# The sums of w_ada moved from GpSimd and ScalarE to VectorE in a two-layer diffusion backbone

## The chip, the cores and the metric

The kernel runs on one core of a Trainium2 chip. The metric is the device time of one execution in microseconds (us); the median of three runs before the change is 1243.5 us (1242.24 to 1245.1). TensorE (PE) does the matrix products, VectorE (DVE), ScalarE (ACT) and GpSimd (POOL) the element work, and SyncE (SP) issues most DMA transfers. Each engine takes its instructions from its own queue, in order.

## The reference

Two layers run over 512 latent tokens of width 1024. Layer 0 mixes tokens by attention and a Fourier transform, layer 1 by a conformer convolution module; each layer ends with a gated feed-forward part of width 2816 with a short convolution. Before each part the tokens are normalised, scaled and shifted, and behind it they are gated. The six vectors of each layer that scale, shift and gate come from one conditioning vector:

```
def ada_params(cond, w_ada_i, b_ada_i):
    m = jax.nn.silu(cond) @ w_ada_i + b_ada_i
    ...
    return jnp.split(m, 6, axis=-1)
...
        x_lat = x_lat + g1 * o_lat
        h = modulate(rmsnorm(x_lat, g_ffn[i]), sh2, sc2)
        x_lat = x_lat + g2 * conv_ffn(h, w_up[i], w_fdw[i], b_fdw[i], w_down[i])
```

`silu(cond) @ w_ada` is a product of one row with a 1024 x 6144 matrix for each layer. The kernel reads w_ada from HBM in tiles of 128 x 1024: a tile holds 128 output columns, one for each partition, and along its free dimension all 1024 inputs. Multiplied by silu(cond), which stands in every partition (tile `scb`), and summed along the free dimension, one tile gives 128 values of one vector; eight tiles give a vector.

## The kernel before, in words

**Weights.** All other weights come as 174 chunks of 128 x 1024 (`Stream`). The DMA of a chunk goes to one of two stage tiles `st`; ScalarE rounds it to its high part `whi` (L195), and VectorE takes the low part `wlo = st - whi` (L196). Five chunks are held at a time, so chunk n+5 is made when TensorE is done with chunk n. A product takes three matmuls (`mm3`, L223 to L225): high by high, high by low, low by high. A chunk is 24 matmuls of 512 columns. The text calls chunks by their number in this stream, which is also the number in the names `whi33`, `wlo33`.

**The feed-forward part of layer 0, ffn(0).** Chunks 18 to 21 are its first block. Then come, for each i, two "up" chunks (22 and 23, 24 and 25, 26 and 27, 29 and 30, ...), whose results TensorE puts into PSUM banks `B`, of which there are four in rotation. Every second i has a "down" chunk between (28, 33, 38, ...), whose results gather in the wide tiles `D`. When an up chunk is done, `conv` runs on its bank: one pass on ScalarE (L923) and two on VectorE (L924, L925); the second VectorE pass frees the bank for the up chunk four banks later. `glu` multiplies the two halves (L933), and a down chunk needs the result g split into a high part (ScalarE, L290) and a low part (VectorE, L291). Behind chunk 32 the gate takes two banks of the rotation, so that chunk 34 gets the bank of chunk 31 and chunk 35 that of chunk 32.

**The sums.** `ada_sum` loads a tile of w_ada into `sa` (three buffers, SyncE queue), GpSimd multiplies it by `scb` in place (L384), and ScalarE sums each half along the row (L387, two instructions, each followed by a read of its accumulator). At the end VectorE adds the pairs and the bias (L390, L391). 40 tiles run in ffn(0), 8 in the conformer part, 8 in ffn(1), always as fillers beside the products. A gate is wanted in every row: `in_every_row` spreads a vector by 8 small matmuls on TensorE (L369), four into each of two banks, and ScalarE copies each bank out (L370).

**The conformer part.** Up chunks 84 to 99 are followed by a convolution by transforms; among it two tiles `bp` of a bias are loaded into the same two stage tiles `st` as the weights, multiplied on GpSimd by the gate, and added to x by eight GpSimd instructions (L1143), after which the stage tiles are free again.

**What sets the order.** The program is written in loops with fillers, but the framework's scheduler puts the instructions of each engine into a fixed order when the program is built. So the order of a queue is settled before the run, and an instruction that is not ready holds all behind it.

## Time and profile before

| | before |
|---|---|
| median of the runs | 1243.5 us |
| profiled execution | 1242.08 us, span 1240.3 us |
| TensorE busy | 1172.2 us (95%) |
| VectorE busy | 764.1 us (62%) |
| ScalarE busy | 588.1 us (47%) |
| GpSimd busy | 260.3 us (21%), of it 153.9 us on the 56 multiplications L384 |

The profile gives each engine's instructions with start and duration, what an engine waited for, and the granted clock of TensorE as a share of full speed (PEclk). Busy shares are averages; the stretches that matter here are 300 to 450 us (ffn(0) with 40 sums), 690 to 765 us (conformer with 8) and 895 to 930 us (ffn(1) with 8).

### The profile page before, as it was taken

The page shows a single profiled execution, that of the slowest core. Times are in us where ns is not written, and L with a number is a line of the kernel's source. Part 1 is how long each engine was busy: PE and PEld are TensorE (multiplying, and loading weights), DVE is VectorE, ACT ScalarE, POOL GpSimd, SP SyncE. Part 2 cuts the span into 40 slices and gives each one's busy share as a digit, 9 for nine tenths or more (in the row PEclk, how much of TensorE's full clock was granted, in tenths as well). Part 3 has the DMA queues.
Part 4 walks back from the last instruction along what each step waited for, and adds up shares of the span by engine and source line. Part 5 has one row for each costly group of instructions (what it writes and reads, how often), then busy time and mean ns, then how long its engine had stood idle before and what let it go on. Part 6 is the DMA issues. An engine that isn't in the chain of part 4 may idle for free.

```text
span 1240.3 us, 15425 instructions
## 1 busy us (share of the span) xinstructions
PE 1172.2 (95%) x5813; PEld 962.7 (78%) x5813; DVE 764.1 (62%) x1092; ACT 588.1 (47%) x1021; POOL 260.3 (21%) x164
## 2 busy tenths in 40 slices
PE   4899899999996999999999999979999999999998
PEld 1686477769885888888888877868988888888886
DVE  3458599346987667554646675664686545555563
ACT  4454587325766664334444543342574433433441
POOL 2025255001677830000001650000250000000000
PEclk8999999999998999999999998989999999999999
DMA  9534600222666653222234443101264232232230
GB/s 361 219 135 160 204 1 1 99 105 86 244 224 238 228 206 133 100 89 101 86 102 154 156 139 105 55 17 51 86 207 132 85 103 88 99 102 92 95 119 34
DMA packets 43834, 156.43 MB, mean 126 GB/s; under 512 B 5008, under 2 KB 5520, under 8 KB 43504
## 3 DMA queue, kind: packets, MB, share of 16 engines
q1 hardware_dynamic: 42192, 149.51, 34.9%
q0 software_dynamic: 1120, 5.54, 1.3%
q8 instruction: 46, 0.75, 0.2%
q10 hardware_dynamic: 448, 0.39, 0.1%
q14 instruction: 28, 0.23, 0.1%
HBM read 153.33 MB, written 2.10 MB: 125 GB/s over the span
## 4 chain that ended last, share of the span: by engine, by line
PE 73%; DVE 10%; DMA 7%; ACT 4%; issue 3%; POOL 2%; SPq 0%; POOLq 0%; ACTq 0%; DVEq 0%
PE B L223 17%; PE B L224 16%; PE B L225 16%; PE D L223 6%; PE D L224 6%; PE D L225 6%; DVE wlo L196 3%; DMA sa<-in_wada_dram 3%; DMA st<-in_wall_dram 2%; POOL sa L384 2%; PE B L829 2%; PE B L338 1%; DMA wn<-in_wnat_dram 1%; DVE tiny L809 1%; ACT P L812 1%
## 5 line engine op out<-in xcount | busy, mean ns | idle before, releaser
L196 DVE TENSOR_TENSOR wlo<-st,whi 128x1024 fp32r<-128x1024 f32 x174 | 239.2, 1378 | 245.0 <-ACT whi L195 242.0
L223 PE MATMUL B<-h,whi 128*128 128x512 f32 (+1 forms) x880 | 313.8, 370 | 10.9 <-DVE tmp L925 8.8
L224 PE MATMUL B<-h,whi 128*128 128x512 f32 (+1 forms) x880 | 321.8, 369 | 0.0
L225 PE MATMUL B<-h,wlo 128*128 128x512 f32 (+1 forms) x880 | 320.3, 368 | 0.0
L195 ACT CAST whi<-st 128x1024 fp32r<-128x1024 f32 x174 | 182.1, 1049 | 177.2 <-PE B L224 101.7
L223 PEld LDWEIGHTS B<-h,whi 128*128 128x128 f32 x880 | 162.3, 190 | 39.2 <-issue 9.4
L224 PEld LDWEIGHTS B<-h,whi 128*128 128x128 f32 x880 | 167.2, 190 | 26.8
L225 PEld LDWEIGHTS B<-h,wlo 128*128 128x128 f32 x880 | 166.8, 190 | 27.1
L384 POOL TENSOR_TENSOR sa<-sa,scb 128x1024 f32<-128x1024 f32 x56 | 153.9, 2767 | 79.1 <-DMA sa<-in_wada_dram 39.1
L290 ACT CAST g<-g 128x512 fp32r<-128x512 f32 x88 | 54.6, 621 | 153.6 <-DVE g L933 74.4
L287 POOL TENSOR_TENSOR tiny<-tiny,mhalf 128x1 f32<-128x1 f32 (+3 forms) x26 | 21.2, 816 | 462.4 <-DVE tiny L286 461.2
L291 DVE TENSOR_TENSOR g<-g,g 128x512 fp32r<-128x512 f32 x88 | 69.9, 795 | 71.4 <-ACT g L290 71.4
L387 ACT ACTIVATE sa<-sa 128x512 f32<-128x512 f32 x112 | 69.5, 624 | 30.3 <-POOL sa L384 30.1
L224 PE MATMUL D<-wlo,g 128*128 128x512 f32 x176 | 68.5, 389 | 0.0
L225 PE MATMUL D<-whi,g 128*128 128x512 f32 x176 | 68.5, 389 | 0.0
L223 PE MATMUL D<-whi,g 128*128 128x512 f32 x176 | 68.5, 389 | 0.0
L223 PE MATMUL B<-whi,g 128*128 128x512 f32 x176 | 68.5, 389 | 0.0
L224 PE MATMUL B<-wlo,g 128*128 128x512 f32 x176 | 68.5, 389 | 0.0
L225 PE MATMUL B<-whi,g 128*128 128x512 f32 x176 | 67.8, 389 | 0.0
L924 DVE SCALAR_TENSOR_TENSOR tmp<-B,vecs,tmp 128x511 f32<-128x511 f32 x84 | 62.1, 743 | 5.3 <-ACT tmp L923 5.3
L931 ACT ACTIVATE tmp<-tmp 128x512 f32<-128x512 f32 x44 | 27.8, 631 | 77.9 <-DVE tmp L925 77.1
L923 ACT ACTIVATE tmp<-B,vecs 128x512 f32<-128x512 f32 x84 | 64.4, 771 | 0.0
(239 smaller groups left out, 1919.5 us busy)
## 6 DMA issues: line engine op xcount, KB each, us to landing
st<-in_wall_dram SPq DMA_DIRECT2D x174, 512.0 KB, 3.5
sa<-in_wada_dram SPq DMA_DIRECT2D x56, 512.0 KB, 4.4
wn<-in_wnat_dram SPq DMA_DIRECT2D x24, 512.0 KB, 9.3
sa<-in_wnat_dram SPq DMA_DIRECT2D x16, 512.0 KB, 4.8
x<-in_x_dram SPq DMA_DIRECT2D x4, 512.0 KB, 5.2
dft<-in_dft_dram POOLq DMA_DIRECT2D x2, 1024.0 KB, 6.9
out_dram<-x SPq DMA_DIRECT2D x8, 256.0 KB, 2.0
scb<-in_cond_dram SPq DMA_DIRECT2D x3, 512.0 KB, 5.7
```

The costliest lines, as they stand in the source:

```text
L195: nc.scalar.copy(hi, st)
L196: nc.vector.tensor_tensor(out=lo, in0=st, in1=hi, op=ALU.subtract)
L223: nc.tensor.matmul(out, lhsT=lh, rhs=rh, start=start, stop=False)
L224: nc.tensor.matmul(out, lhsT=lh, rhs=rl, start=False, stop=False)
L225: nc.tensor.matmul(out, lhsT=ll, rhs=rh, start=False, stop=stop)
L290: nc.scalar.copy(hi, src)
L291: nc.vector.tensor_tensor(out=lo, in0=src, in1=hi, op=ALU.subtract)
L384: nc.gpsimd.tensor_tensor(out=st, in0=st, in1=cur["c"], op=ALU.mult)
L387: nc.scalar.activation(out=u, in_=u, func=AF.Identity, accum_out=acc[:, 2 * kt + i : 2 * kt + i + 1])
L923: nc.scalar.activation(out=y, in_=b, func=AF.Identity, scale=w[:, 1:2], bias=vec(f"bfdw{l}", i))
L924: nc.vector.scalar_tensor_tensor(out=y[:, 1:SEQ], in0=b[:, 0 : SEQ - 1], scalar=w[:, 0:1], in1=y[:, 1:SEQ], op0=ALU.mult, op1=ALU.add)
L931: nc.scalar.activation(out=sa, in_=ya, func=AF.Silu)
```

## The change

GpSimd no longer takes part. For each tile of w_ada one VectorE instruction multiplies it by `scb` and sums along the row (`scalar_tensor_tensor` with `accum_out`, L384 after). ScalarE's two sums per tile go, and so does the pairwise addition L390. `acc` has 8 columns and six buffers. A gate is spread in two steps of the filler, one bank each.

```
-    def in_every_row(col, dst):
-        for half in range(2):
+    def in_every_row(col, dst, halves=(0, 1)):
+        for half in halves:
...
-        acc = tp.tile([P, KT * 2], F32, tag="asum", name=nm("asum"), bufs=3)
+        acc = tp.tile([P, KT], F32, tag="asum", name=nm("asum"), bufs=6)
         for kt in range(KT):
             st = chunk_tile()
             nc.sync.dma_start(st, wada[(6 * l + j) * KT + kt])
-            nc.gpsimd.tensor_tensor(out=st, in0=st, in1=cur["c"], op=ALU.mult)
-            for i in range(2):
-                u = st[:, i * 512 : i * 512 + 512]
-                nc.scalar.activation(out=u, in_=u, func=AF.Identity, accum_out=acc[:, 2 * kt + i : 2 * kt + i + 1])
+            nc.vector.scalar_tensor_tensor(out=st, in0=st, scalar=1.0, in1=cur["c"], op0=ALU.mult, op1=ALU.mult, accum_out=acc[:, kt : kt + 1])
             yield
         col = tiny(8)
-        nc.vector.tensor_reduce(out=col, in_=acc.rearrange("p (k s) -> p k s", s=2), op=ALU.add, axis=AX.X)
-        nc.vector.tensor_tensor(out=col, in0=col, in1=vec("ba", (6 * l + j) * KT, KT), op=ALU.add)
+        nc.vector.tensor_tensor(out=col, in0=acc, in1=vec("ba", (6 * l + j) * KT, KT), op=ALU.add)
         yield col
...
-                in_every_row(col, dst)
+                in_every_row(col, dst, (0,))
+                yield
+                in_every_row(col, dst, (1,))
```

The scheduler's order changes with it. After the change every line from L396 on has a number lower by two (L924, L925, L933 and L1143 before are L922, L923, L931 and L1141 after).

VectorE at the start of the sums in ffn(0), before: low parts of chunks 23 to 26 and the conv passes of the first block (banks B_624 to B_626).

```order
L196 TENSOR_TENSOR wlo23_2996<-st23_2997,whi23_2995 128x1024
L924 SCALAR_TENSOR_TENSOR tmp_628_3019<-B_624_2799,vecs_70,tmp_628_3019 128x511
L196 TENSOR_TENSOR wlo24_3002<-st24_3003,whi24_3001 128x1024
L925 SCALAR_TENSOR_TENSOR tmp_628_3019<-B_624_2799,vecs_70,tmp_628_3019 128x511
L924 SCALAR_TENSOR_TENSOR tmp_630_3025<-B_625_2800,vecs_70,tmp_630_3025 128x511
L924 SCALAR_TENSOR_TENSOR tmp_631_3030<-B_626_2801,vecs_70,tmp_631_3030 128x511
L925 SCALAR_TENSOR_TENSOR tmp_630_3025<-B_625_2800,vecs_70,tmp_630_3025 128x511
```

The same place after, with the sums (sa, asum) among them:

```order
L384 SCALAR_TENSOR_TENSOR sa_639_3114,asum_638_3113<-sa_639_3114,scb_621_2794 128x1024
L384 SCALAR_TENSOR_TENSOR sa_640_3117,asum_638_3113<-sa_640_3117,scb_621_2794 128x1024
L384 SCALAR_TENSOR_TENSOR sa_646_3193,asum_638_3113<-sa_646_3193,scb_621_2794 128x1024
L196 TENSOR_TENSOR wlo23_2996<-st23_2997,whi23_2995 128x1024
L922 SCALAR_TENSOR_TENSOR tmp_628_3019<-B_624_2799,vecs_70,tmp_628_3019 128x511
L196 TENSOR_TENSOR wlo24_3002<-st24_3003,whi24_3001 128x1024
L384 SCALAR_TENSOR_TENSOR sa_647_3196,asum_638_3113<-sa_647_3196,scb_621_2794 128x1024
L384 SCALAR_TENSOR_TENSOR sa_659_3312,asum_638_3113<-sa_659_3312,scb_621_2794 128x1024
L923 SCALAR_TENSOR_TENSOR tmp_628_3019<-B_624_2799,vecs_70,tmp_628_3019 128x511
L384 SCALAR_TENSOR_TENSOR sa_660_3315,asum_638_3113<-sa_660_3315,scb_621_2794 128x1024
```

Three sums now stand ahead of chunk 23's low part, and further ones between each pair of the old instructions.

VectorE further on in ffn(0), after: the second conv pass on bank B_668 (chunk 31) and what stands between it and that on B_669 (chunk 32), which comes twelve rows later. These are the banks that chunks 34 and 35 take over.

```order
L923 SCALAR_TENSOR_TENSOR tmp_674_3497<-B_668_3397,vecs_70,tmp_674_3497 128x511
L384 SCALAR_TENSOR_TENSOR sa_797_4777,asum_770_4498<-sa_797_4777,scb_621_2794 128x1024
L931 TENSOR_TENSOR g32_622_2797<-tmp_664_3384,tmp_665_3386 128x512
L196 TENSOR_TENSOR wlo38_3492<-st38_3493,whi38_3491 128x1024
L384 SCALAR_TENSOR_TENSOR sa_840_5147,asum_839_5146<-sa_840_5147,scb_621_2794 128x1024
L387 TENSOR_TENSOR tiny_807_4891<-asum_770_4498,vecs_70 128x8
L922 SCALAR_TENSOR_TENSOR tmp_676_3503<-B_669_3398,vecs_70,tmp_676_3503 128x511
L291 TENSOR_TENSOR g_693_3669<-g32_622_2797,g_692_3668 128x512
L384 SCALAR_TENSOR_TENSOR sa_845_5188,asum_839_5146<-sa_845_5188,scb_621_2794 128x1024
L196 TENSOR_TENSOR wlo39_3549<-st39_3550,whi39_3548 128x1024
L384 SCALAR_TENSOR_TENSOR sa_850_5229,asum_839_5146<-sa_850_5229,scb_621_2794 128x1024
```

The next two rows are the first conv pass of chunk 34 and then the second of chunk 32, the 35th sum being the last one ahead of them. In the order of before no sum stands on this engine.

TensorE in ffn(0), after: the end of chunk 29, then part of down chunk 33, then chunk 30. Before, chunk 30 follows chunk 29 at once, and all of chunk 33 stands behind chunk 32.

```order
L223 MATMUL B_661_3318<-h_5_86,whi29_3146 128x512
L224 MATMUL B_661_3318<-h_6_87,whi29_3146 128x512
L225 MATMUL B_661_3318<-h_5_86,wlo29_3147 128x512
L223 MATMUL D_654_3269<-whi33_3295,g_670_3459 128x512
L223 MATMUL D_655_3270<-whi33_3295,g_670_3459 128x512
L224 MATMUL D_654_3269<-wlo33_3296,g_670_3459 128x512
L225 MATMUL D_654_3269<-whi33_3295,g_671_3460 128x512
```

Half of chunk 33 (12 matmuls) has moved ahead of chunk 30, and with it the moment at which its low part is wanted; six matmuls of chunk 28 have likewise moved ahead of chunk 27, and the other 18 stand where all 24 stood.

## Rows read from the trace of the kernel before

**Rows 1.** The page, parts 5 and 2: the multiplications, and GB/s in 40 slices.

```profile
L384 POOL TENSOR_TENSOR sa<-sa,scb 128x1024 f32<-128x1024 f32 x56 | 153.9, 2767 | 79.1 <-DMA sa<-in_wada_dram 39.1
...
GB/s 361 219 135 160 204 1 1 99 105 86 244 224 238 228 206 133 100 89 101 86 102 154 156 139 105 55 17 51 86 207 132 85 103 88 99 102 92 95 119 34
```

**Rows 2.** Windows: length, busy us (instructions) PE PEld DVE ACT POOL, PEclk, DMA, GB/s.

```profile
375.00:400.00 25.00, 16.59 (x71) 13.57 (x70) 19.26 (x14) 17.16 (x43) 20.76 (x8) 0.80 0.62 214
...
725.00:750.00 25.00, 22.58 (x109) 18.81 (x108) 18.48 (x29) 10.48 (x16) 4.82 (x4) 0.93 0.41 145
750.00:775.00 25.00, 22.02 (x110) 18.73 (x109) 13.64 (x21) 9.63 (x15) 0.00 (x0) 0.86 0.28 91
...
900.00:925.00 25.00, 25.00 (x112) 20.68 (x112) 22.10 (x24) 20.57 (x44) 14.99 (x6) 1.00 0.65 225
```

**Rows 3.** TensorE's waits, 290 to 460 us: us in total, times, longest.

```profile
PE B L223 <- DVE tmp L925: 8.8, 2, 8.4
```

**Rows 4.** Timeline, TensorE: first matmuls of chunks 29, 33, 34, 39 (start, duration).

```profile
345.12 0.39 PE L223 MATMUL B<-h,whi 128*128 128x512 f32 x1
...
366.88 0.39 PE L223 MATMUL D<-whi,g 128*128 128x512 f32 x1
...
383.98 0.77 PE L223 MATMUL B<-h,whi 128*128 128x512 f32 x1 [8.41 <-DVE tmp L925]
...
412.62 0.39 PE L223 MATMUL B<-h,whi 128*128 128x512 f32 x1
```

**Rows 5.** VectorE's groups by form, 305 to 445 us: busy us, mean ns.

```profile
L196 DVE TENSOR_TENSOR wlo<-st,whi 128x1024 fp32r<-128x1024 f32 x23 | 48.8, 2121 | 27.4 <-ACT whi L195 27.4
L933 DVE TENSOR_TENSOR g<-tmp,tmp 128x512 f32<-128x512 f32 x10 | 16.7, 1669 | 0.2
L291 DVE TENSOR_TENSOR g<-g,g 128x512 fp32r<-128x512 f32 x9 | 14.1, 1562 | 3.0 <-ACT g L290 3.0
```

**Rows 6.** The same by form, 460 to 640 us, where GpSimd is idle.

```profile
L196 DVE TENSOR_TENSOR wlo<-st,whi 128x1024 fp32r<-128x1024 f32 x35 | 42.8, 1225 | 50.4 <-ACT whi L195 47.6 <-PE B L369 2.8
L291 DVE TENSOR_TENSOR g<-g,g 128x512 fp32r<-128x512 f32 x29 | 20.0, 691 | 24.7 <-ACT g L290 24.7
```

**Rows 7.** Timeline, VectorE in ffn(0).

```profile
330.57 1.21 DVE L196 TENSOR_TENSOR wlo<-st,whi 128x1024 fp32r<-128x1024 f32 x1
331.70 0.74 DVE L924 SCALAR_TENSOR_TENSOR tmp<-D,vecs,tmp 128x511 f32<-128x511 f32 x1
332.47 0.75 DVE L925 SCALAR_TENSOR_TENSOR tmp<-D,vecs,tmp 128x511 f32<-128x511 f32 x1
333.14 2.00 DVE L196 TENSOR_TENSOR wlo<-st,whi 128x1024 fp32r<-128x1024 f32 x1
...
383.08 0.75 DVE L925 SCALAR_TENSOR_TENSOR tmp<-B,vecs,tmp 128x511 f32<-128x511 f32 x1
```

**Rows 8.** Timeline, ScalarE: scb made ready, and an accumulator read.

```profile
303.87 1.06 ACT L308 ACTIVATE scb<-scb 128x1024 f32<-128x1024 f32 x1
...
309.50 0.19 ACT L387 ACTIVATION_READ_ACCUMULATOR sa<-sa 128x1 f32 x1
309.59 0.62 ACT L387 ACTIVATE sa<-sa 128x512 f32<-128x512 f32 x1
```

**Rows 9.** Timeline in the conformer part: GpSimd's last additions to x; VectorE beside them.

```profile
723.57 6.25 POOL L1143 TENSOR_TENSOR x<-x,bp 128x512 f32<-128x512 f32 x4
...
725.24 3.44 DVE L291 TENSOR_TENSOR z<-tmp,z 128x512 fp32r<-128x512 f32 x2
```

**Rows 10.** Waits, 720 to 765 us, of TensorE and of ScalarE.

```profile
PE D L224 <- DVE z L291: 2.4, 2, 1.6
PE B L223 <- ACT V L1088: 1.9, 1, 1.9
...
ACT whi L195 <- DMA st<-in_wall_dram: 9.6, 5, 3.4
```

**Rows 11.** Tile sa: its DMAs' time to landing.

```profile
DMA to landing us min/median/max: 3.3/4.5/9.6
```

## The prediction, made before the changed kernel ran

> **What bounds the kernel now.** I read the page first: TensorE is busy for 95% of the span, so only its pauses can be won or lost. The windows and TensorE's waits then say where these lie and whether the sums have to do with them. In ffn(0) one window holds 16.6 us of matmuls in 25 us, at 0.80 of the clock [rows 2]; the wait list has one large entry, 8.4 us on VectorE's L925 [rows 3]. The timeline places it: chunk 34 cannot start until 383.98 [rows 4], right behind the conv pass that ends at 383.83 [rows 7] and frees its bank. So the limit there is how soon VectorE gets through its queue. What slows that queue is seen in the groups by form: beside the sums a low part takes 2121 ns, a product L933 1669 and a split L291 1562 [rows 5]; where GpSimd is idle the first takes 1225 and the other tile size 691 [rows 6]. All three read two SBUF tiles, as GpSimd's multiplication does; the conv passes, which read PSUM, take 0.74 beside the sums too [rows 7]. In the conformer part two windows together lack 5.4 us of TensorE work, at 0.93 and 0.86 of the clock [rows 2]; the entries are splits z of VectorE and copies V of ScalarE [rows 10]. In ffn(1) TensorE is full although VectorE works 22.1 us of 25 [rows 2].
>
> **The change, ffn(0).** Removed: 40 GpSimd multiplications, and with them the stretching of VectorE. By rows 5 and 6 that gives VectorE back 23 x 0.90 + 10 x 0.98 + 9 x 0.87 = 38 us. Added: 40 sums on VectorE. Their price is not in the trace. From below it is a low part, which reads the same two tiles of 1024 columns: 1.14 us from start to start (330.57 to 331.70) [rows 7]; a gain on that is excluded, since no row of VectorE with two SBUF sources beats that pace. From above I add a whole accumulator read as ScalarE shows it, 0.19 us, so 1.33; ScalarE's next instruction starts 0.09 us after its read starts [rows 8], so I take 1.14 + 0.10 = 1.24. Forty cost 50 us, so VectorE's work grows by about 12 us, and the question is where in the queue it stands. ScalarE's 80 half sums go too, but ScalarE is not what TensorE waits for here.
>
> I therefore walk VectorE's queue as the order after the change has it, from the first sum at 304.9, when scb is ready [rows 8], with 1.24 a sum, 1.14 a low part, 0.70 a conv pass (steps of 0.77 and 0.67 in rows 7), 0.61 a half tile (691 ns less the overlap of 0.08 that low parts show) and 0.16 for a tiny one. Ahead of and with four instructions stand:
> - second conv pass of chunk 21: 13 sums, 7 low parts, 9 passes, 2 half tiles, 1 tiny: done at 336.7;
> - low part of the second g for chunk 28: 16, 9, 13, 4, 1: 346.7;
> - low part of chunk 33: 21, 11, 16, 6, 3: 358.8;
> - second conv pass of chunk 31: 31, 15, 26, 10, 5: 385.5, and of chunk 32: 35, 17, 29, 12, 6: 396.3.
>
> TensorE needs 5.44 us a chunk (345.12 to 366.88 for four, rows 4). Before, it reached chunk 29 at 345.12 without a pause. After, chunk 27 wants its bank 1.1 us before it is free; chunk 28's second half then stands ready at 343.5 and waits until 346.7 (3.2 us); chunk 29 waits 0.5 us for a bank (17 sums ahead: 349.9) and ends at 355.4. Now comes the half of chunk 33 that has moved ahead of chunk 30: it wants its low part and waits until 358.8 (3.4). With chunks 30, 31, 33's rest, 32 and the gate TensorE is through at 382.4, waits for chunk 31's pass until 385.5 (3.1), runs chunk 34 to 390.9 and waits for chunk 32's pass until 396.3 (5.4). Four chunks later chunk 39 would start at 418.0. Of the clock only the loss behind the last pause counts, as the earlier ones end in the next wait; before, the five chunks from 383.98 to 412.62 took 28.6 instead of 27.2 us [rows 4], so 1.4. Chunk 39 starts at 419.4 instead of 412.6: **ffn(0) loses 6.8 us**. The sums are behind by then and I charge nothing more. With 1.14 the same walk gives +3.2, with 1.33 +10.2.
>
> Hidden in this: the tiles sa. Three sums of the queue take 3 x 91.4 / 35 = 7.8 us, and a buffer has to be reloaded within that less the sum itself (1.24) and its issue (about 0.4): 6.2 us, where a landing takes 4.5 [rows 11]. If that cover goes, see the rivals. SyncE's queue mixes these loads with chunks; the order puts three of them ahead of chunk 25's, and each is issued as its sum ends.
>
> **The change, conformer.** The sums leave GpSimd, where they stood before and between the additions to x; these end at 729.8 [rows 9] and hold the two stage tiles of the weight stream. After, GpSimd has only the bias and the additions. The bias tiles load about 4 us later than before, since the two low parts that free their stages stand behind six sums (7.4 us) but no longer wait for GpSimd (3.2 us); with 2.5 us of multiplication and 2 x 5.6 us of additions GpSimd is done near 725. So the weights restart some 5 us earlier, ScalarE's 9.6 us of waits for them shrink and with them the 1.9 us for V. The splits z, 3.44 us for two behind GpSimd's additions [rows 9], fall partly beside them still. The pauses are worth 5.4 us and the clock, by its shares, at most 1.8 + 3.5 us of which some lies in the pauses: 9.5 us in all. I take 6, with 0 and 9.5 as bounds: **the conformer gains 6 us**.
>
> **The change, elsewhere.** In ffn(1) the queue has 8 sums ahead of the pass that chunk 27 waited for in the walk, five fewer, so it is done 6 us earlier than there, 5 us ahead of TensorE: 0, hidden by that lead; if it were gone, 1 us per us. The gates in halves are the same 16 matmuls and two copies; one stands three chunks later, under matmuls, far ahead of its use: 0, or about 2 us if TensorE waited for them.
>
> **Sum.** 1242.1 + 6.8 - 6 = 1242.9 for the profiled execution, which lies 1.4 us under the median: **1244 us**.
>
> **The rivals.**
> - *VectorE frees TensorE more than it costs* (faster). The sum costs no more than a low part (ffn(0) +3.2) and all of the conformer's pauses go (-9.5): 1237 us. For it speaks that VectorE's own work hardly grows and ScalarE's falls; against it the two places where a pass now stands behind 31 and 35 sums.
> - *The sums wait for their tiles* (slower). A sum whose tile has not landed holds low parts and conv passes behind it. In the walk 52 tiles of 0.52 MB pass in 91 us, 298 GB/s, where the same stretch now moves 206 to 244 and the whole kernel's peak slice 361 [rows 1]. It decides once a landing exceeds 6.2 us; then each us over it comes once in three sums, 35/3 = 11.7 us by chunk 35. Landings reach 9.6 [rows 11]. At 6.9 it is 8 us: 1252.
> - *VectorE runs this form at half pace* (slower). No row shows a multiply-and-sum with two SBUF sources and 1024 columns; the wide ones in the trace have one source in PSUM. If 512 columns took twice the 0.53 us that separates a half tile from a whole one, a sum would take 2.3 us, chunk 32's pass would end at 433, chunk 39 start 42 us later than before, and the other parts add some 5: 1290. Against it speaks that low parts, also two fp32 SBUF sources, keep full pace [rows 6].
>
> The Trainium skill, Vector Engine (DVE) Microarchitecture Reference, section 7 (Points that are easy to get wrong), says that the scalar-tensor-tensor form with two SBUF sources that are not bf16 runs at half throughput. By that rule the time would be the 1290 of the last rival; nothing in this trace shows the form, and the two-source rows that it does show are not halved.
>
> **How the numbers follow.** A measurement of this kernel can tell about 0.2%, 2.5 us, from no change. Forecast (both terms near each other, 1237 to 1254 by its bounds): 0.47, of which within 0.2% 0.27, faster 0.07, slower 0.13. First rival 0.24, faster. Second 0.20, slower. Third 0.09, slower. So faster 0.31, same 0.27, slower 0.42. The range from 1235 to 1258 leaves out the third rival, the worst of the second and the best of the first, 0.19 together; the forecast's own range is 1239 to 1250.
>
> **What would show it.** Right: VectorE's low parts in 305 to 445 fall to about 1.23 us; a sum takes 1.2 to 1.35 us; TensorE's wait list there has several pauses of 3 to 5 us on L923 and wlo instead of one of 8.4, 16 us in all; GpSimd's additions end near 725 and the wait on V is gone. Wrong: sums of 2.2 us (half pace); VectorE waiting for sa tiles by more than a few us in sum (second rival); fewer than 10 us of pauses in ffn(0), which would say that the queue walk is too slow; pauses left as they are in the conformer.

## The result, and the profile after

The changed kernel takes 1228.13 us (median, 1227.57 to 1230.13) where the kernel before takes 1243.7: a ratio of 0.9878, 95% interval 0.9861 to 0.9895. By the medians it is 15.6 us faster; the prediction had 1244 and a range that began at 1235. The profiled execution of after took 1230.13 us, span 1228.4, and is the slowest of its four.

The first thing to make is a table of stages. The start of a chunk's first matmul on TensorE's timeline marks the stages well, since each stage so cut holds the same number of matmuls in every run; the last one ends with TensorE's last matmul, 4.8 us before the span does. All times in us:

| from chunk to chunk | stage | before | after | difference |
|---|---|---|---|---|
| start to 22 | mixer, first block | 298.4 | 301.9 | +3.5 |
| 22 to 39 | ffn(0) with most sums | 114.2 | 110.1 | -4.1 |
| 39 to 84 | rest of ffn(0) | 251.2 | 250.6 | -0.6 |
| 84 to 100 | conformer | 159.5 | 148.9 | -10.6 |
| 100 to TensorE's last matmul | second half, ffn(1) | 412.2 | 412.0 | -0.2 |

The first stage holds nothing of the change: up to chunk 22 TensorE's order is that of before. Over the runs below whose program is the same there it scatters from 298 to 303 us (306 in e18, whose tiles are moved), while the others repeat within about 1 us where nothing in them was changed. So the profiled execution hides 3.5 us; without its first stage the sum is -15.4, close to the difference of the medians. In the rows below everything in ffn(0) lies 3.5 us later than it would in the execution of before.

VectorE by form in 305 to 445 us, after (answers to [rows 5]; columns: busy us, mean ns, idle time ahead):

```profile
L384 DVE SCALAR_TENSOR_TENSOR sa<-sa,scb 128x1024 f32<-128x1024 f32 x40 | 48.0, 1216 | 2.2 <-ACT scb L308 1.4 <-DMA sa<-in_wada_dram 0.8
L196 DVE TENSOR_TENSOR wlo<-st,whi 128x1024 fp32r<-128x1024 f32 x26 | 31.7, 1218 | 10.3 <-ACT whi L195 10.3
...
L931 DVE TENSOR_TENSOR g<-tmp,tmp 128x512 f32<-128x512 f32 x11 | 7.5, 684 | 0.1
L291 DVE TENSOR_TENSOR g<-g,g 128x512 fp32r<-128x512 f32 x11 | 7.5, 682 | 2.1 <-ACT g L290 2.1
```

The low parts fell from 2121 to 1218 ns, products and splits from 1669 and 1562 to 684 and 682. A sum takes what a low part takes. The timeline of VectorE at the first sums shows that reading the accumulator costs nothing: the next sum starts with the read.

```profile
308.42 1.23 DVE L384 SCALAR_TENSOR_TENSOR sa<-sa,scb 128x1024 f32<-128x1024 f32 x1 [1.41 <-ACT scb L308]
309.57 0.08 DVE L384 DVE_READ_ACCUMULATOR sa<-sa,scb 128x1 f32 x1
309.57 1.22 DVE L384 SCALAR_TENSOR_TENSOR sa<-sa,scb 128x1024 f32<-128x1024 f32 x1
310.72 0.08 DVE L384 DVE_READ_ACCUMULATOR sa<-sa,scb 128x1 f32 x1
```

From start to start it is 1.15 us. What is left of TensorE's waits in 290 to 460 us, after (answers to [rows 3]; us in total, times, longest):

```profile
PE D L223 <- DVE tmp L923: 2.7, 1, 2.7
PE D L224 <- DVE wlo L196: 2.1, 1, 2.1
PE B L223 <- DVE h L448: 0.7, 1, 0.7
```

The first is the second half of chunk 28, the second the part of chunk 33 that moved ahead of chunk 30. The pause of 8.4 us ahead of chunk 34 is gone. Windows of after (answers to [rows 2]; columns as there):

```profile
325.00:350.00 25.00, 22.29 (x98) 17.89 (x97) 25.00 (x39) 11.18 (x14) 0.00 (x0) 1.00 0.90 313
350.00:375.00 25.00, 22.93 (x94) 18.50 (x93) 25.00 (x43) 9.64 (x14) 0.00 (x0) 0.93 0.86 289
375.00:400.00 25.00, 25.00 (x120) 20.99 (x119) 24.22 (x37) 9.58 (x13) 0.00 (x0) 1.00 0.89 304
725.00:750.00 25.00, 24.58 (x135) 21.02 (x134) 18.18 (x30) 12.15 (x17) 0.00 (x0) 1.00 0.50 170
750.00:775.00 25.00, 25.00 (x130) 21.37 (x129) 14.18 (x27) 7.71 (x12) 0.00 (x0) 1.00 0.17 56
900.00:925.00 25.00, 25.00 (x112) 20.71 (x111) 22.97 (x32) 15.66 (x22) 0.00 (x0) 1.00 0.41 139
```

In ffn(0) VectorE is now full, at 24 to 25 us of 25, and TensorE still gets most of what it wants. In the conformer part the two windows that lacked 5.4 us lack 0.4, and the granted clock is 1.00 where it was 0.93 and 0.86. GpSimd's additions there end at 721.6 us (answers to [rows 9]), and of ScalarE's 9.6 us of waits for weights in 720 to 765 us 7.9 remain (answers to [rows 10]). The two splits z that took 3.44 us beside the additions in before now start 0.7 us behind the last addition and take 1.46 us:

```profile
711.02 10.61 POOL L1141 TENSOR_TENSOR x<-x,bp 128x512 f32<-128x512 f32 x8
...
722.28 1.46 DVE L291 TENSOR_TENSOR z<-tmp,z 128x512 fp32r<-128x512 f32 x2
```

```profile
ACT whi L195 <- DMA st<-in_wall_dram: 7.9, 5, 2.1
```

### The profile page after: what moved, and what is told of

Read it like the earlier page. It is cut to its first block, busy times and chain, and to the rows that moved or that the text cites. A ratio compares the mean times of both kernels' runs of the same rounds, so it can differ in the third digit from the quotient of the medians.

```text
span 1228.4 us, 15185 instructions
## 1 busy us (share of the span) xinstructions
PE 1169.3 (95%) x5813; PEld 958.2 (78%) x5813; DVE 766.8 (62%) x1197; ACT 519.3 (42%) x797; POOL 104.7 (9%) x108
## 4 chain that ended last, share of the span: by engine, by line
PE 81%; DVE 9%; DMA 4%; ACT 3%; issue 2%; SPq 0%; POOL 0%; ACTq 0%; DVEq 0%; POOLq 0%
PE B L223 19%; PE B L224 18%; PE B L225 18%; PE D L224 6%; PE D L223 6%; PE D L225 6%; DMA st<-in_wall_dram 2%; DVE wlo L196 2%; PE B L827 2%; PE B L338 2%; DMA wn<-in_wnat_dram 1%; DVE tiny L807 1%; DVE sa L384 1%; ACT P L810 1%; PE B L822 1%
## 5 line engine op out<-in xcount | busy, mean ns | idle before, releaser
L196 DVE TENSOR_TENSOR wlo<-st,whi 128x1024 fp32r<-128x1024 f32 x174 | 212.2, 1223 | 234.8 <-ACT whi L195 234.6
L291 DVE TENSOR_TENSOR g<-g,g 128x512 fp32r<-128x512 f32 x88 | 60.7, 690 | 69.1 <-ACT g L290 69.1
L384 DVE SCALAR_TENSOR_TENSOR sa<-sa,scb 128x1024 f32<-128x1024 f32 x56 | 67.0, 1217 | 2.6 <-ACT scb L308 1.4
L923 DVE SCALAR_TENSOR_TENSOR tmp<-B,vecs,tmp 128x511 f32<-128x511 f32 x84 | 62.4, 747 | 2.1
L922 DVE SCALAR_TENSOR_TENSOR tmp<-B,vecs,tmp 128x511 f32<-128x511 f32 x84 | 62.1, 743 | 0.0
```

Source lines behind the costliest of these rows:

```text
L196: nc.vector.tensor_tensor(out=lo, in0=st, in1=hi, op=ALU.subtract)
L291: nc.vector.tensor_tensor(out=lo, in0=src, in1=hi, op=ALU.subtract)
L384: nc.vector.scalar_tensor_tensor(out=st, in0=st, scalar=1.0, in1=cur["c"], op0=ALU.mult, op1=ALU.mult, accum_out=acc[:, kt : kt + 1])
L922: nc.vector.scalar_tensor_tensor(out=y[:, 1:SEQ], in0=b[:, 0 : SEQ - 1], scalar=w[:, 0:1], in1=y[:, 1:SEQ], op0=ALU.mult, op1=ALU.add)
L923: nc.vector.scalar_tensor_tensor(out=y[:, 0 : SEQ - 1], in0=b[:, 1:SEQ], scalar=w[:, 2:3], in1=y[:, 0 : SEQ - 1], op0=ALU.mult, op1=ALU.add)
```

## The experiments

Three questions came up: do the parts of the change add up, what frees TensorE in ffn(0), and what does so in the conformer. Stage lengths (us) from the profiled execution of each run, and medians. The ratio to before is a 95% interval against the kernel before run beside it, whose median lay between 1241.7 and 1243.7 us:

| run | 22 to 39 | 39 to 84 | 84 to 100 | 100 to TensorE's last | median | ratio to before |
|---|---|---|---|---|---|---|
| before | 114.2 | 251.2 | 159.5 | 412.2 | 1243.7 | 1 |
| after | 110.1 | 250.6 | 148.9 | 412.0 | 1228.1 | 0.986 to 0.990 |
| e1 gate in one step | 110.7 | 250.6 | 148.7 | 412.0 | 1229.9 | 0.987 to 0.990 |
| e2 ffn(0) alone, tiles moved | 110.2 | 257.3 | 158.3 | 419.7 | 1253.4 | 1.007 to 1.010 |
| e3 conformer alone, tiles moved | 113.2 | 257.0 | 149.1 | 420.0 | 1248.4 | 1.003 to 1.005 |
| e4 before, gate one pair later | 123.6 | 250.5 | 158.9 | 412.0 | 1250.9 | 1.005 to 1.008 |
| e5 ffn(0) alone | 110.6 | 250.6 | 158.5 | 412.2 | 1238.8 | 0.996 to 0.999 |
| e6 conformer alone | 114.2 | 250.5 | 148.4 | 412.0 | 1233.2 | 0.991 to 0.996 |
| e7 GpSimd busy in ffn(0) | 142.3 | 250.5 | 148.7 | 412.0 | 1261.3 | 1.014 to 1.018 |
| e8 GpSimd busy in the conformer | 110.4 | 250.6 | 165.3 | 412.2 | 1245.7 | 1.001 to 1.004 |
| e9 stage tiles held long | 110.5 | 250.6 | 165.2 | 412.1 | 1244.0 | 1.000 to 1.002 |
| e10 tiles moved by 192 bytes | 109.6 | 257.3 | 149.7 | 420.2 | 1246.4 | 1.002 to 1.004 |
| e11 two tiles sa | 102.9 | 250.6 | 152.4 | 412.0 | 1233.4 | 0.990 to 0.994 |
| e12 ScalarE's share back | 115.3 | 250.6 | 148.9 | 412.0 | 1240.5 | 0.997 to 0.999 |
| e13 stage tiles held as before | 110.9 | 250.6 | 154.3 | 412.2 | 1233.4 | 0.992 to 0.995 |
| e14 ScalarE's share back, later | 108.3 | 250.6 | 148.9 | 412.0 | 1226.3 | 0.986 to 0.990 |
| e15 two tiles sa in ffn alone | 102.9 | 250.6 | 148.8 | 412.0 | 1221.9 | 0.982 to 0.986 |
| e16 banks as predicted | 111.7 | 250.5 | 149.5 | 412.0 | 1230.3 | 0.989 to 0.993 |
| e17 tiles moved by 64 bytes | 109.9 | 256.2 | 149.1 | 420.3 | 1243.8 | 1.0005 to 1.0035 |
| e18 tiles moved by 128 bytes | 111.4 | 256.9 | 150.0 | 422.8 | 1248.0 | 1.003 to 1.007 |

**e1, the gate in one step.**

```
-                in_every_row(col, dst, (0,))
-                yield
-                in_every_row(col, dst, (1,))
+                in_every_row(col, dst)
```

> The kernel after, with one thing undone: a gate is spread in one step again, both halves together; the sums stay on VectorE. In the trace of after, chunk 35 started at 390.5 us although chunk 32's second conv pass ended only at 396.0: chunks 34 and 35 took the banks that the gate had left, not those of chunks 31 and 32. Theory A (the scheduler gives out the bank that its plan sees free first, and VectorE's load in the plan decides that; the halves have no part in it): chunk 35 takes a gate bank here too, time 1228 us, within 1 us of after. Theory B (the split of the gate is what freed a bank early): chunk 35 waits 5.5 us for chunk 32's pass, time 1233 to 1234.

It took 1229.9 us, ffn(0) 0.5 us longer than after. Theory A held: by the medians the halves are worth nothing that can be measured. The program's waits show the banks. The first matmul of chunk 35 waits for VectorE and ScalarE before, for ScalarE alone after and in e1:

```
before  L223 MATMUL B_683_3546<-h_3_84,whi35_3386 128x512 [waits DVE_49,Activation_49]
after   L223 MATMUL B_681_3523<-h_3_84,whi35_3374 128x512 [waits Activation_49]
```

The trace of after, chunk 35's start on TensorE and the conv pass of chunk 32 on VectorE, says the same: it starts 5.5 us before that pass ends.

```profile
390.47 0.39 PE L223 MATMUL B<-h,whi 128*128 128x512 f32 x1
```

```profile
395.26 0.74 DVE L923 SCALAR_TENSOR_TENSOR tmp<-B,vecs,tmp 128x511 f32<-128x511 f32 x1
```

So what was said ahead of the prediction, that chunks 34 and 35 take over the banks of chunks 31 and 32, holds for the kernel before alone; after the change they take the gate's.

**e2 and e3, one part alone.** `ada_sum` got both bodies, chosen by vector, with a second tag for the old partial sums:

```
+        if (l, j) not in ((1, 4), (1, 5)):      # e3: if (l, j) == (1, 4):
+            acc = tp.tile([P, KT], F32, tag="asum", name=nm("asum"), bufs=6)
...
+        else:
+            acc = tp.tile([P, KT * 2], F32, tag="asum2", name=nm("asum"), bufs=3)
```

> Only the 40 sums of ffn(0) on VectorE, the 16 of the conformer part and ffn(1) on GpSimd and ScalarE as before; gates in halves. Theory A (as measured by the chunks' starts, ffn(0) gains 4.8 us from chunk 22 to chunk 65, the conformer the other 10.5): 1238.5 to 1240. The prediction's own step (ffn(0) loses 6.8): 1250. A third reading, that the parts are not independent (the conformer gains because ffn(0) ends in another state): under 1236.

> Only the 8 sums of the conformer part on VectorE, the 40 of ffn(0) and the 8 of ffn(1) as before; gates in halves. Theory A (the conformer gives the whole of its pauses and of its lost clock, 10.5 us, by itself): 1232 to 1234. The prediction's step (6 us): 1237 to 1238. The halves alone would show as a change in ffn(0), where theory A expects none (the 8.4 us pause ahead of chunk 34 stays).

Both came out slower than before, 1253.4 and 1248.4 us, which no theory had. The table shows why it is not the sums: the stages that hold nothing of what they change are 6 to 8 us longer too. A 512-column matmul step had gone from 227 to 233 ns (median start to start, 470 to 640 us) in the whole kernel, because the second tag moved the tiles behind it, h and g among them (e10 below shows the move alone). So the times of e2 and e3 say nothing on the change.

**e5 and e6, the same with addresses kept.** One tag of 3 x 64 bytes serves both bodies:

```
+        acc = tp.tile([P, KT * 2], F32, tag="asum", name=nm("asum"), bufs=3)
+        if (l, j) not in ((1, 4), (1, 5)):      # e6: if (l, j) == (1, 4):
+            acc = acc[:, 0:KT]
```

> As e2 (only the 40 sums of ffn(0) on VectorE), but with one thing put right: in e2 and e3 a second tag for the partial sums moved the tiles behind it, h among them, by 192 bytes, and every 512-column matmul step became 233 ns instead of 227 over the whole kernel. Here asum keeps the 192 bytes that before and after give it, so h and all tiles stay where they are. Theory A (ffn(0) gains 4 to 5 us by itself, the drift of e2 came from the addresses): steps of 227 ns and 1238.5 to 1240. Theory B (the parts are not independent, and ffn(0) alone loses): 1250 and more, with steps of 227 ns.

> As e3 (only the 8 sums of the conformer part on VectorE), with the addresses kept as in e5. Theory A (the conformer gives 10 to 10.5 us by itself): steps of 227 ns, 1232.5 to 1234, and the pause of 8 us ahead of chunk 34 still there. The prediction's step: 1237.5. Theory B of e5: above 1243.

Steps of 227 ns. e5 gains 3.6 us in ffn(0) and keeps the conformer nearly as before; e6 gains 11.1 in the conformer and keeps ffn(0), where TensorE's wait on the conv pass is 7.7 us. Theory A held: by the stages the parts are independent and add up to after (3.6 + 11.1 = 14.7, and 4.1 + 10.6 in after). The medians are too coarse for that sum: against the kernel before run beside them e5 gains 2.9 and e6 8.5 us, 11.4 of the 15.6, with intervals of some 2 and 3 us to either side. In e6, with the gate in halves and the old sums in ffn(0), chunk 34 still waits for chunk 31's pass; with e1 that says that the sums on VectorE, not the halves, moved the banks.

**e4, the gate of before one pair later.**

```
                 if (l, j) == (0, 5):
                     yield
                     yield
                 in_every_row(col, dst)
```

> The kernel before, with one thing changed: the gate of ffn(0) is spread one pair of up chunks later, so that chunks 34 and 35 take the banks of 29 and 30, the gate those of 31 and 32, and chunk 36 that of chunk 34. Theory A (the 8.4 us pause was a matter of which bank chunk 34 was given): chunk 34 starts at about 375.6 instead of 384 and the time falls to about 1236. Theory B (VectorE's queue, stretched beside GpSimd, is late by as much whatever bank is taken): the pause moves to chunk 36, which now waits for chunk 34's conv pass, and the time stays at 1243 to 1245.

It took 1250.9 us. Theory A fell, and B was too mild: chunk 34 starts early, but the waits come back larger. TensorE's timeline of e4, the gate and chunk 36:

```profile
392.71 2.04 PE L369 MATMUL B<-ident,tiny 128*128 128x128 f32 x8 [5.35 <-DVE tmp L928]
...
406.27 0.77 PE L223 MATMUL B<-h,whi 128*128 128x512 f32 x1 [11.51 <-DVE tmp L928]
```

So before the change VectorE's queue was late whichever bank one looks at; the bank only says where it shows, and how much of it.

**e7, GpSimd busy in ffn(0) again.** After, and for each of the first 24 sums:

```
+            nc.gpsimd.tensor_tensor(out=gate1, in0=cur["c"], in1=cur["c"], op=ALU.mult)
```

> The kernel after with 24 additional GpSimd multiplications of scb by itself (128x1024 fp32, two SBUF sources, into a tile that is not in use), one for each of the first 24 sums of ffn(0); no other engine's order changes and nobody waits for them. Theory A (what the change takes away in ffn(0) is the stretching of VectorE beside GpSimd, which pays for the sums): beside them a sum and a low part take about 2.1 us instead of 1.2, VectorE's queue falls 30 us or more behind within their 66 us, and TensorE's pauses grow by as much: 1255 to 1270. Theory B (the stretching costs little now, the gain comes from ScalarE's and the order's relief): within 2 us of after, 1228 to 1230.

ffn(0) lost 32 us. VectorE by form in 305 to 375 us, e7:

```profile
L384 DVE SCALAR_TENSOR_TENSOR sa<-sa,scb 128x1024 f32<-128x1024 f32 x15 | 39.6, 2662 | 1.4 <-ACT scb L308 1.4
L196 DVE TENSOR_TENSOR wlo<-st,whi 128x1024 fp32r<-128x1024 f32 x8 | 18.3, 2282 | 0.0
```

Nobody waits for these multiplications, and no other queue's order differs. So with GpSimd busy beside 24 of them the sums cost 32 us more than in after. What the change takes away in ffn(0) is this stretching, and that pays for the sums: theory A. The kernel before without GpSimd's multiplications and without sums on VectorE was not run, so the relief and the price of the sums are measured only together.

**e12 and e14, ScalarE busy again.** After, and for the same 24 sums two instructions (e12 on `gate1` in place, e14 reading `scb`):

```
+                for i in range(2):
+                    nc.scalar.activation(out=gate1[:, i * 512 : i * 512 + 512], in_=cur["c"][:, i * 512 : i * 512 + 512], func=AF.Identity, accum_out=modA[:, kt, 0:1])
```

> The kernel after with ScalarE's half sums back for the first 24 sums of ffn(0) (48 instructions with accumulator, on a tile that is not in use); nobody waits for them. It is the pair of e7, which brought GpSimd's share back for the same 24 sums and lost 33 us. Theory A (only GpSimd's share cost TensorE time; ScalarE's relief is worth nothing): within 2 us of after, 1227 to 1230. Theory B (ScalarE's relief is a good part of the gain): 1231 to 1235.

> As e12, with the 48 half sums of ScalarE reading scb, so that they cannot start before it is ready at 308 us. In e12 they stood ready earlier and half of its 10 us were lost before the sums began (chunks 18 to 22). Theory A (ScalarE's relief in ffn(0) is worth nothing): chunks 22 to 39 take no longer than in after, 1227 to 1230. Theory B (it is worth about what e12 lost from chunk 22 on): 5 us more, 1232 to 1234.

e12 lost 12 us, but five of them ahead of the sums: its instructions, ready early, stood 27 strong in ScalarE's queue between 280 and 312 us. e14, where they wait for scb, took 1226.3 us with ffn(0) 1.8 shorter than after, although ScalarE worked 24.7 us of 25 in its first window:

```profile
325.00:350.00 25.00, 22.73 (x94) 18.08 (x93) 25.00 (x38) 24.72 (x62) 0.00 (x0) 0.93 0.89 295
```

So the gain in ffn(0) doesn't need ScalarE's relief. More isn't shown: in e12 and e14 the scheduler's order differs from after on every queue but GpSimd's (in e14 TensorE takes 2 matmuls of chunk 33 ahead of chunk 30 instead of 12), and e12's other 5 us (ffn(0) 115.3) weren't followed up. ScalarE's 16 half sums of the conformer part were not put back in any run.

**e16, the banks that the prediction assumed.** The gate's banks are read once more when chunk 32's conv is done:

```
             nc.scalar.copy(dst[:, half * 512 : half * 512 + 512], b)
+            if cur.get("y") is not None:
+                nc.vector.tensor_tensor(out=tiny(1), in0=b[:, 0:1], in1=cur["y"][:, 0:1], op=ALU.add)
```

> The kernel after with the gate's two banks of ffn(0) held until chunk 32's conv passes are done (two VectorE instructions on one column read them then), so that chunks 34 and 35 take the banks of chunks 31 and 32, as the prediction had it. The order moves most of down chunk 38 (22 of 24 matmuls, 5 us) ahead of chunk 35. Theory A (the scheduler fills such a wait with other matmuls, and the prediction was wrong to charge it): within 1.5 us of after, 1227 to 1230. Theory B (chunk 35 waits for chunk 32's pass as predicted): 5.5 us more, 1233 to 1235.

1230.3 us, ffn(0) 1.6 longer than after. Chunk 35 does not wait for its bank: with 22 matmuls of chunk 38 ahead of it, it starts at 397.9 us, 2.2 us after chunk 32's pass has ended (395.6). What is lost lies ahead of chunk 34, which starts 0.5 us after chunk 31's pass (386.96) and, counted from chunk 22, 2.1 us later than in after; two matmuls of chunk 38 stand ahead of it and wait for their weights (TensorE's timeline of e16):

```profile
386.86 0.73 PE L223 MATMUL D<-whi,g 128*128 128x512 f32 x2 [1.59 <-ACT whi L195]
```

The order has filled the wait of chunk 35. That is theory A, though 1.6 us and the 1230.3 lie just past its bounds.

**e8, GpSimd busy in the conformer.** After, and behind the additions to x:

```
+            for _ in range(8):
+                nc.gpsimd.tensor_tensor(out=ytm[:, :, 768:1024], in0=x[:, TT - 1, :]..., in1=x[:, TT - 2, :]..., op=ALU.mult)
```

> The kernel after with 8 additional GpSimd multiplications (128x1024 fp32, two SBUF sources) right behind the additions to x in the conformer part, from about 722 to 742 us; no other engine's order changes and nobody waits for them. They stretch VectorE, but hold no stage tile. Theory A (the conformer gained because GpSimd gives the two stage tiles back 8 us earlier and the weight stream restarts): the gain stays, 1228 to 1230. Theory B (it gained because the splits z and the low parts are no longer stretched): 3 to 6 us are lost again, 1231 to 1234.

16.3 us lost, more than either theory had. VectorE by form in 722 to 745 us, first e8, then after:

```profile
L196 DVE TENSOR_TENSOR wlo<-st,whi 128x1024 fp32r<-128x1024 f32 x3 | 9.5, 3203 | 0.0
...
L1107 DVE TENSOR_TENSOR tmp<-tmp 128x256 f32<-128x256 f32 x2 | 5.1, 2560 | 0.0
```

```profile
L196 DVE TENSOR_TENSOR wlo<-st,whi 128x1024 fp32r<-128x1024 f32 x7 | 8.6, 1223 | 6.1 <-ACT whi L195 6.1
...
L1107 DVE TENSOR_TENSOR tmp<-tmp 128x256 f32<-128x256 f32 x2 | 0.8, 420 | 0.0
```

An instruction of 0.42 us became 2.56 in the mean: it lost 2.1 us, as much as the low part of 1.22. A division of pace would have stretched both by one factor; a wait for most of a GpSimd instruction (22.20 us for the eight, 2.78 each) fits better. The Trainium skill, SBUF — State Buffer, section "SBUF: two separate sides", says so of VectorE instructions with two SBUF inputs beside GpSimd's: "The shared pair is an exclusive lock, not a bandwidth split". The trace agrees in these two groups, 2.1 and 2.0 us lost.

**e9 and e13, the stage tiles held longer, GpSimd not busier.** After, with the load of each bias tile repeated on GpSimd's DMA queue, three times (e9) or once (e13):

```
                 nc.sync.dma_start(bp, bpw2[c : c + 512].partition_broadcast(P))
+                for _ in range(3):
+                    nc.gpsimd.dma_start(bp, bpw2[c : c + 512].partition_broadcast(P))
```

> The kernel after, with the loads of the two bias tiles bp repeated three times on GpSimd's DMA queue, one behind the other, so that GpSimd's multiplication and additions come some 8 us later and hold the two stage tiles as long as before the change, while GpSimd computes no more than after. The order of some conformer instructions on TensorE moves with it. Theory A (in the conformer the change gained by giving the stage tiles back earlier, as the prediction has it): 4 to 6 us are lost again, 1232 to 1234. Theory B (it gained by no longer stretching VectorE; e8 bears it out from the other side): within 2 us of after, 1227 to 1230.

> As e9, with one repeated load of each bias tile instead of three. In e9 the additions to x ended at 735.9 us instead of 721.6, 14.3 us later, and 16.4 us were lost in the conformer part, so that holding the stage tiles does cost time there and theory B of e9 fell; before the change the additions ended 8.2 us later than after. Here they should end 5 to 7 us later. If TensorE has no slack the loss is as large, 5 to 8 us (1233 to 1236), and the hold explains most of the conformer's 10.6 us; if there is a slack of some us, as the wait of e9 (a chunk late by 11) would also allow, it is 0 to 3 us (1228 to 1231), and the hold explains little of it.

GpSimd's additions and VectorE's two splits z in e13, then in e9:

```profile
714.37 11.84 POOL L1143 TENSOR_TENSOR x<-x,bp 128x512 f32<-128x512 f32 x8
...
721.62 3.44 DVE L291 TENSOR_TENSOR z<-tmp,z 128x512 fp32r<-128x512 f32 x2
```

```profile
725.20 10.67 POOL L1143 TENSOR_TENSOR x<-x,bp 128x512 f32<-128x512 f32 x8
...
719.69 1.47 DVE L291 TENSOR_TENSOR z<-tmp,z 128x512 fp32r<-128x512 f32 x2
```

Counted from the start of chunk 84 (662.6 us in after, 660.6 in e13, 663.8 in before, 662.9 in e9) the additions end after 59.1, 65.6, 66.0 and 73.0 us. The conformer takes 148.9, 154.3, 159.5 and 165.2 us. So e13 holds the tiles as long as before did and loses 5.4 us; e9 holds them 13.9 us longer than after and loses 16.3. Theory B of e9 fell: a long enough hold costs time though the splits z are not stretched, and TensorE then waits for the high part of chunk 93, the first chunk whose load waits for these tiles (e9):

```profile
PE B L223 <- ACT whi L195: 4.8, 1, 4.8
```

But e13 does not measure the hold alone. Its later additions lie over the splits z as before the change, and these take 3.44 us again; the one wait of TensorE there that e13 has and after hasn't is for them, and its clock in 720 to 730 us is 0.67 where after has 1.00:

```profile
PE D L224 <- DVE z L291: 2.3, 2, 2.0
```

```profile
720.00:730.00 10.00, 7.72 (x32) 6.21 (x32) 8.72 (x10) 2.28 (x3) 6.20 (x4) 0.67 0.40 115
```

For chunk 93's weights TensorE has no wait in e13. So the 5.4 us are those of hold and stretched splits together, and the wait that TensorE shows is for the splits. The other 5.2 us of before have no run to explain them; e8 shows what stretching alone can cost there. e9 and e13 also move some 35 of the 5701 matmuls in TensorE's order.

**e10, e17, e18, the tiles moved.** After, with another number of buffers of 32 bytes for the partial sums; no engine's order changes:

```
-        acc = tp.tile([P, KT], F32, tag="asum", name=nm("asum"), bufs=6)
+        acc = tp.tile([P, KT], F32, tag="asum", name=nm("asum"), bufs=12)      # e17: 8, e18: 10
```

> The kernel after with twelve buffers for the partial sums instead of six. No engine's order changes; the tiles behind them (h among them) lie 192 bytes higher, as in e2 and e3. Theory A (the address of h alone made the matmul steps 233 instead of 227 ns there): steps of 233 ns, and 174 chunks of 24 steps x 6 ns = 25 us less what falls into pauses, 1245 to 1254. Theory B (the mixed code of e2 and e3 did it in another way): 1228 to 1230.

> The kernel after with eight buffers for the partial sums: the tiles behind them lie 64 bytes higher instead of the 192 of e10; no engine's order changes. Theory A (any move off the address that before and after share slows the matmul steps): 233 ns and 1243 to 1248. Theory B (64 bytes is still an address that TensorE reads at full pace): 227 ns and 1227 to 1230.

> The same with ten buffers, 128 bytes higher. Theory A: 233 ns and 1243 to 1248. Theory B (128 bytes is an address at full pace, 192 is not): 227 ns and 1227 to 1230.

Theory A in all three: steps of 233, 233 and 232 ns, and 1246.4, 1243.8 and 1248.0 us. In 500 to 525 us TensorE is full, at full clock, in e10 and in after, and gets through 109 and 112 matmuls:

```profile
500.00:525.00 25.00, 25.00 (x109) 20.19 (x108) 13.98 (x17) 8.82 (x12) 0.00 (x0) 1.00 0.31 91
```

```profile
500.00:525.00 25.00, 25.00 (x112) 20.72 (x111) 14.53 (x17) 9.49 (x13) 0.00 (x0) 1.00 0.26 92
```

The change keeps 6 x 32 = 192 bytes where 3 x 64 stood. Had it kept three buffers of 32 bytes, the tiles would have moved too; that size wasn't run.

**e11 and e15, fewer tiles for the sums.** e11 gives the tag `sa` two buffers; e15 only for the sums of the feed-forward parts:

```
     def chunk_tile():
-        return wp.tile([P, D], F32, tag="sa", name=nm("sa"), bufs=3)
+        ns[0] += 1
+        third = cur.get("all3", True) and ns[0] % 3 == 0      # all3 is False in ffn
+        return wp.tile([P, D], F32, tag="sb" if third else "sa", name=nm("sa"), bufs=1 if third else 2)
```

> The kernel after with two buffers for the w_ada tiles instead of three, so that the sums of ffn(0) are spread over a longer stretch (the 40th stands where VectorE's queue comes to about 419 instead of 404 us) and VectorE gets to its conv passes and low parts sooner in 325 to 375 us. Theory A (the 4.8 us of pauses that are left in ffn(0) come from sums standing ahead of the old instructions): they go, 1224 to 1226. Theory B (with two buffers a sum waits for its tile, and all behind it on VectorE with it): over 5 us of waits for sa tiles, 1229 to 1236.

> The kernel after with the sums of the feed-forward parts on two of the three w_ada buffers; all else keeps the three (in e11 the mixer part lost 9.2 us by having two, and the conformer 3.5, while ffn(0) caught up 7.2). Theory A (in ffn(0) the later sums leave VectorE in time for its conv passes and low parts): no pauses in ffn(0), 1221 to 1224, better than both kernels. Theory B (e11's catching up was only the slack of a late start): 1227 to 1229.

e11 loses 9 us in the mixer and 3.5 in the conformer, but ffn(0) takes 102.9 us. e15 keeps that alone: 1221.86 us (1219.24 to 1224.41), ratio 0.9839, 0.9819 to 0.986, some 5 us faster than after by the two ratios (0.9878 - 0.9839 = 0.0039 of 1243) and faster than both kernels. Its windows and waits in ffn(0):

```profile
325.00:350.00 25.00, 25.00 (x112) 20.71 (x111) 24.35 (x36) 13.11 (x18) 0.00 (x0) 1.00 0.82 263
350.00:375.00 25.00, 25.00 (x112) 20.71 (x111) 23.58 (x38) 9.49 (x14) 0.00 (x0) 1.00 0.82 268
375.00:400.00 25.00, 25.00 (x120) 20.97 (x119) 22.59 (x35) 11.15 (x15) 0.00 (x0) 1.00 0.82 260
```

```profile
DVE sa L387 <- DMA sa<-in_wada_dram: 7.8, 12, 1.3
```

TensorE has no pause left, at full clock, although VectorE now waits 7.8 us for tiles. With fewer tiles the sums are spread, so fewer of them stand ahead of a conv pass that TensorE needs: 8 instead of 13 ahead of chunk 21's second pass and 23 instead of 35 ahead of chunk 32's. That VectorE waits somewhere cost TensorE nothing. TensorE's order is another too (chunk 28 stands whole behind chunk 27 again, and of chunk 33 2 matmuls instead of 12 ahead of chunk 30); what each of the two is worth wasn't separated.

## Why the prediction was wrong, point by point

The two parts were charged +0.8 us together and came to -15.4. Of that distance the price of a sum is 3.6 us, the waits of chunks 34 and 35 7.3, the conformer 4.6, and small terms the rest.

**What bounds the kernel**: right. TensorE's pauses were what there was to win, and VectorE's stretched queue made the one in ffn(0) (e7, e4); with ScalarE's load put back no such pause came (e14, though in another order).

**The price of a sum**: mis-sized. I took 1.24 between 1.14 and 1.33, adding half of ScalarE's accumulator read [rows 8]; it was 1.14 to 1.15, the lower bound, since VectorE's read of 0.08 us runs under the next instruction. Over the 35 sums ahead of chunk 32's pass that is 3.5 us, about the step from +6.8 to the +3.2 that the prediction gave for 1.14.

**The queue walk**: right, with that price. It puts chunk 31's pass at 385.5 - 31 x 0.1 = 382.4 and chunk 32's at 392.8; measured, less the late start of 3.5, are 381.6 and 392.5. Also right: the waits for chunk 28's second half (3.2 predicted, 2.7 by the walk at 1.14, 2.7 measured) and for chunk 33's low part (3.4, 3.1, 2.1). The prediction had named fewer than 10 us of pauses in ffn(0) as the sign of a walk that is too slow. 5.5 us came, and the sign misled: the walk held, and it was the use made of it for chunks 34 and 35 that failed.

**The waits of chunks 34 and 35** (3.1 and 5.4 us): the step that failed. I carried the bank rotation of before over: chunk 34 gets chunk 31's bank and 35 that of 32. With the sums in VectorE's queue the scheduler gave them the gate's two banks, freed by ScalarE's copies, as e1 and e5 have it too, and chunk 35 ran 5.5 us before chunk 32's pass was done. (That it gives out the bank which its plan sees free first fits this, and e6, but was not tested by itself.) The order of after showed it, had I read which engine the first matmul of each chunk waits for rather than bank names. And e16 says that with the assumed banks the charge would still have been too high, 1.6 us in all, since the order then puts 22 matmuls of chunk 38 into the wait of chunk 35. By the walk at 1.14 the two waits are 2.1 and 5.0 us, nearly all of the 7.3 us from +3.2 to the measured -4.1.

**The conformer**: right that GpSimd's share held TensorE up there (e6), short in size, and the division was wrong. The 6 us were argued from the hold of the stage tiles, and the stretching was let go with "fall partly beside them still". In after the splits z fall behind the additions altogether and take 1.46 us instead of 3.44, and e13, which brings hold and stretched splits back together, loses 5.4 us with its only added wait on the splits. How the 10.6 us divide between hold, stretching and clock stays open. The upper bound of 9.5 us, all pauses and the clock, was the better value, and 10.6 lies even beyond it.

**ffn(1) and the gates**: 0 and 0 predicted; -0.2 us from chunk 100 on, and 0.5 us for the halves in e1.

**The rivals**: the first (1237) named both of the things that happened, and still charged 3.2 us for ffn(0). The second did not come: VectorE waited 0.8 us for sa tiles in 300 to 450 us, at 289 to 313 GB/s; landings took 4.8 us in the median. The third fell with the first sum: 1.22 us. The rule of the Trainium skill named beside it (Vector Engine (DVE) Microarchitecture Reference, section 7, two fp32 SBUF sources at half throughput) does not hold for this form here: a sum takes as long as a low part of the same size, which also has two fp32 SBUF sources but no accumulator.

## What to carry to other kernels

Where two engines stretch each other, cost a move from the price of the pair: e7's 24 instructions that nobody waited for cost 32 us. When you put a piece back to measure it, look at what else it lies over: e13's later additions brought a second cause back with the first. Before charging a wait for a buffer, read in the new order which engine releases it, since the scheduler may hand buffers out anew with a change on another engine. And when an edit adds or resizes a small tile, compare the matmul step in a stage that it doesn't touch before believing the total.

## What the runs showed of the hardware

- Moving the tiles behind the partial sums by 64, 128 or 192 bytes lengthened a 512-column matmul step from 227 to 232 or 233 ns here (e10, e17, e18); e11, in which h lies 4096 bytes lower, has 227. Over the stage from chunk 39 to 84 that is 5.6 to 6.7 us of 250.6, and in the medians 16 to 20 us, as much as the whole change gains. Which of the tiles does it was not tried.
- A multiply-and-sum on VectorE with two fp32 SBUF sources, 128x1024, takes 1.22 us, 1.15 from start to start, and its accumulator read of 0.08 us is hidden.
- Beside GpSimd's instructions on two SBUF tiles a short VectorE instruction of the same kind lost as much in the mean as a long one (0.42 to 2.56 us, 1.22 to 3.20, e8), while those with a PSUM source kept their time: conv passes took 738 ns beside them in e7, 742 in after.
